# A two-layer mixer on one core: 128-row products in place of 32-column ones for the gate weights and the second layer's shift and scale, and a 128-row broadcast of the running maximum

## Chip, core and metric

The kernel runs on one core of a Trainium2 chip. The metric is the time of one execution on the device, in microseconds (us); for the kernel before the median of three runs is known. Besides that there is the trace of one profiled execution. The engines are named as in the profile: PE (TensorE, its products), PEld (TensorE, its weight loads), DVE (VectorE), ACT (ScalarE), POOL (GpSimd), SP (SyncE, which issues all DMAs of this kernel).

## What is computed

Two layers of a mixer over 512 tokens and 1024 channels, all in float32. Each layer normalises x, scales and shifts it by vectors that come from a condition c (`mod`), projects it to five groups of 1024 columns, runs a gated linear recurrence (RG-LRU) on two groups and a chunked mLSTM of four heads on the other three, and projects back. Cut to what the change touches:

```python
mod = c_act @ w_ada[l] + b_ada[l]
shift, scale, gate = jnp.split(mod, 3, axis=-1)
h = rms_norm(x, norm_g[l]) * (1.0 + scale[:, None, :]) + shift[:, None, :]
...
q = block_diag(xc, w_q)          # 4 heads, 256 x 256 each
k = block_diag(xc, w_k)
v = block_diag(xm, w_v)
gates = (jnp.concatenate([q, k, v], axis=-1) @ w_if + b_if)     # 3072 -> 8
...
m_t = jnp.maximum(m_inter, jnp.max(d, axis=-1))                 # running maximum of a head
w_intra = jnp.exp(d - m_t[..., None])
```

## The kernel before

**Precision.** Almost every product is made of three: an operand is split into a high and a low part of the type float32r (`whi` and `wlo` for weights, `hh` and `hl` for activations), and hi*hi, hi*lo and lo*hi are summed in PSUM (`mm3`). A few small products take plain float32 operands (`f32=True`); the trace has two weight loads and two products on PE for each of these.

**Order.** A planner records every instruction in the order in which the program traces it and then makes a list schedule: each engine serves what is due first, by costs and due times that the planner works out from assumed durations. The result is a fixed order on every engine. Each engine then runs its own list strictly in order, and waits where an operand isn't there yet or a buffer isn't free. The tile `raw` (a block of weights as it comes from memory, 512 KB) has three buffers, and the SP queue issues the next load when a buffer is free.

**Gate weights.** The gates need (w_q, w_k, w_v) @ w_if. For each of four heads `qk_weights` makes the tile `A` = w_q w_k^T (12 products of 256 columns), and beside it the gates' weights seen through w_q and w_k: 256 channels by 8. `v_gate_weights` does the same for w_v, two heads at a time. Before, the 8 columns of w_if are the stationary operand, padded with zeros to 32 columns (`wifpad`), and the 256 columns of `raw` are streamed. Four such products fill the four column quarters of the array (`tp=(0, 32 * q)`, tile `wqg` or `wvg`). Then `fold` copies the result to SBUF (`wfsb`, on DVE) and transposes and sums it with two further products by a selection matrix (`sela`, `selg`) into `wfT`, and DVE copies that to `wf`. `wf` is split and put beside other operands: as 8 more columns of `ph`/`pl` (for the scores `S`) and of `wvh`/`wvl` (for the values `v`).

**Second layer's shift and scale.** During `out` and `outq` (the output projection of layer 0) `mod_sum` sums two accumulators (`macc`, 128 rows by 1024 channels) over their rows: four products with 32 columns of ones as stationary operand into the four column quarters (`modps`), a copy (`modsb`), and two products by `sel4` (`modT`).

**Running maximum.** `ml_sw` spreads the running maximum of a head, which lies as hi and lo in rows 0 to 3 and 32 to 35 of `mhl`, over 128 rows by one product with `selh` (tile `Mbc`), using 36 rows of both operands. There are four per layer; two of them stand between products `oz` and two stand ahead of eight transposes `yT`.

**What follows what.** In layer 0 the program traces: `mx` (the mLSTM columns of the input projection), head 0's `qk_weights`, `v_gate_weights`, head 1's `qk_weights`, head 0's `p`, `v` and `S`, head 2's `qk_weights`, the last `mx`, and so on. Layer 1 is alike, with fewer `mx` ahead.

Of the kernel before, what the change touches and what calls it, by code (L numbers as in the profile page):

```python
# [30 lines left out]
# columns of the packed per-channel parameters  # L31
# [3 lines left out]
# what of adaLN is summed up on the vector engine: (layer, third)  # L35
# [3 lines left out]
# order of the rows of w_out: the mLSTM half first  # L39
CORD = list(range(8, 16)) + list(range(0, 8))  # L40
# where block j of the causal scores lies: (tile, first column)
# [4 lines left out]
class View:  # L46
    """A part of a logical tile; becomes an access pattern when its instruction is issued."""
# [60 lines left out]
class Planner:  # L108
    """Records instructions, then issues them on each engine in the order of a list schedule: the tensor
    engine follows the traced order, the others serve what it needs first."""  # L110
# [132 lines left out]
    def deadlines(self):  # L243
# [14 lines left out]
        # a PSUM bank is wanted again by a later tile; ready a little ahead of that  # L258
# [27 lines left out]
    def schedule(self):  # L286
# [4 lines left out]
        ready = {e: [] for e in engines}     # (late, i)  # L291
        events = []                          # (time, i): a finished instruction
        nfree = {k: [(0.0, s) for s in range(n)] for k, (n, _) in self.kinds.items()}
        # tiles still without a slot, by the deadline of their first use
# [18 lines left out]
        def fits(o):  # L313
            need = {}
            for b in o.tiles:
                if b.kind in self.kinds and b.slot is None:
                    need.setdefault(b.kind, []).append(b)
            for k, bs in need.items():
                room = len(nfree[k]) - len(bs)
                if room < 0:  # L320
                    return False
                # slots stay for the tiles that come before these
                ahead, w, h, last = 0, want[k], head[k], max(b.first for b in bs)
                while h < len(w) and w[h][0] < last:
                    if w[h][1].slot is None and w[h][1] not in bs:
                        ahead += 1
                        if ahead > room:
                            return False
                    h += 1
            return True  # L330

        def bank_free(o):
            # engines take turns at a PSUM bank
            return max((b.busy[1] for b in o.tiles if b.kind == "ps" and b.busy[0] != o.eng), default=0.0)
# [23 lines left out]
        while done < len(ops):  # L358
# [23 lines left out]
            # next time at which something changes  # L382
# [43 lines left out]
def trunk_kernel(ctx: ExitStack, tc: tile.TileContext, x, cT, params, bif, bgate, fg,  # L426
# [80 lines left out]
    # t < s: above any maximum, so that its exponential is 0; elsewhere below any  # L507
# [3 lines left out]
    # rows 32 q of four row groups; and pairs of groups, or all, row by row  # L511
    sel4, sel2, selg = keep("sel4", [128, 4]), keep("sel2", [128, 2]), keep("selg", [128, 16])
    sela, selm, selh = keep("sela", [128, 8]), keep("selm", [36, 4]), keep("selh", [36, 4, 128], F32R)

    def selectors():
        P.vcopy(sel4, ident[:, 0:128:32])
        P.tt(sel2, ident[:, 0:128:64], ident[:, 32:128:64], ALU.add)
        for n in range(2):
            P.tt(selg[:, 8 * n:8 * n + 8], ident[:, 64 * n:64 * n + 8], ident[:, 64 * n + 32:64 * n + 40], ALU.add)
        P.tt(sela, selg[:, 0:8], selg[:, 8:16], ALU.add)  # L520
        P.tt(selm, ident[0:36, 0:4], ident[0:36, 32:36], ALU.add)
        P.vcopy(selh, selm.spread(2, 128))
# [31 lines left out]
    def log1p_exp_neg(ab, shape):  # L554
        # log(1 + exp(-ab)) for ab >= 0: u = exp(-ab), 2 atanh(u / (2 + u))
# [23 lines left out]
    # 4 softplus(-lambda), and halves of the biases of the RG-LRU gates, for both layers  # L579
# [18 lines left out]
    def mod_first(d0, nd):  # L598
        # shift and scale of the first layer, channel blocks d0 .. d0 + nd
# [5 lines left out]
        for k in range(4):  # L605
            # quadrants: (which, half of the rows)
# [25 lines left out]
    def mod_units(l, w):  # L632
        # third w (shift, scale, gate) of layer l: products and sums over the blocks of rows, one step a block
# [11 lines left out]
    def mod_sum(l, w):  # L645
        # the sum over the rows of a block
# [14 lines left out]
        ps = bank("modps", (128, 256))  # L661
        for q in range(4):
            P.mm(ps[32 * q:32 * q + 32, :], ones[:, 0:32], acc[q // 2][:, 256 * (q % 2):256 * (q % 2) + 256], True,
                 True, tp=(0, 32 * q), f32=True)
        sb = slot("modsb", F32, (128, 256))
        P.vcopy(sb, ps)
        pt = bank("modT", (128, 4, 2))
        for c in range(2):
            P.mm(pt[:, :, c], sb[:, 128 * c:128 * c + 128], sel4, True, True, f32=True)
        pt = pt.chan(KC)  # L670
# [32 lines left out]
    def h_part(l, hT, xn, d0, nd, half):  # L703
        # channel blocks d0 .. d0 + nd of two token blocks, transposed, scaled, shifted, split
# [48 lines left out]
    def silu2(ps, name, shape=(128, 512)):  # L753
        # 2 silu
        th = slot(name + "t", F32, shape)
        P.act(th, ps, AF.Tanh, scale=0.5)
        P.stt(th, th, 1.0, ps, ALU.add, ALU.mult)
        return th

# [1 line left out]
    def gate_weights(l):  # L761
        raw = slot("wifraw", F32, (128, 24, 8))
        P.dma(raw, w_if[l], 98304)
        pad = [slot("wifpad", F32, (128, 16, 32)), slot("wifpadv", F32, (128, 8, 32))]
        for t, a, b in ((pad[0], 0, 16), (pad[1], 16, 24)):
            P.pool(lambda t=t: nc_g.memset(t.ap(), 0.0), [t], [], 0.4)
            P.vcopy(t[:, :, 0:8], raw[:, a:b, :])
        return pad

    def fold(ps, sel, n):  # L770
        # rows 32 q + g of ps, transposed and summed over the groups q that sel joins: [128, chunk, n]
        sb = slot("wfsb", F32, (128, 256))
        P.vcopy(sb, ps)
        pt = bank("wfT", (128, 2, n))
        for c in range(2):
            P.mm(pt[:, c, :], sb[:, 128 * c:128 * c + 128], sel, True, True, f32=True)
# [4 lines left out]
    def qk_weights(l, p, st):  # L781
        # A = w_q w_k^T, and the gates' weights seen through w_q and w_k
        raw = load_raw(w_qk[l, p], (2, 2, 256))
        ps = bank("wqg", (128, 256))
        for m in range(2):
            for ec in range(2):
                q = 2 * m + ec
                P.mm(ps[32 * q:32 * q + 32, :], st["pad"][0][:, 8 * m + 2 * p + ec, :], raw[:, m, ec, :], True, True,
                     tp=(0, 32 * q), f32=True)
# [9 lines left out]
        st["gq"][p] = fold(ps, sela, 8)  # L799

    def v_gate_weights(l, st):
        for u in range(2):
            raw = load_raw(w_vT[l, u], (2, 2, 256))
            ps = bank("wvg", (128, 256))
            for h in range(2):
                for ec in range(2):
                    q = 2 * h + ec
                    P.mm(ps[32 * q:32 * q + 32, :], st["pad"][1][:, 2 * (2 * u + h) + ec, :], raw[:, h, ec, :],
                         True, True, tp=(0, 32 * q), f32=True)
            st["gv"][u] = fold(ps, selg, 16)  # L810

    def v_weights(l, u, st):
        # w_v of two heads, with the gates' columns beside it
# [24 lines left out]
    def ml_head(l, p, st):  # L838
# [34 lines left out]
        # scores, transposed, times 16; the gates' columns follow the last token  # L873
# [32 lines left out]
    def gate_chain(l, st):  # L906
# [13 lines left out]
        # sums of log f inside the blocks, and the blocks' totals on every partition  # L920
# [4 lines left out]
        # a[i - j][:, j]: log i - b of block j, from where block i starts  # L925
# [23 lines left out]
        P.pool(lambda: nc_g.memset(mhl.ap()[0:36, :].bitcast(F32), 0.0), [mhl[0:36, :]], [], 0.3)  # L949
# [9 lines left out]
    def ml_oz(l, h, hT, st):  # L959
        # tanh(o / 2) and 2 silu(z) of a head, in two steps  # L960
# [19 lines left out]
    def ml_sw(h, st):  # L980
        # S * exp(a_s - M_t), causal, split
        pm = bank("Mbc")
        P.mm(pm, selh[:, h, :], st["mrow"][0:36, :], True, True)
# [74 lines left out]
    def rg_gates(l, g, st):  # L1058
# [4 lines left out]
        for cc in range(2):  # L1063
# [6 lines left out]
            # r2 = 2 sigmoid(p) = (1 + |tanh(p / 2)|) exp(min(p, 0)); s = -log a = 4 sp r2;  # L1070
            # 1 - a^2 = tanh(s) (1 + a^2)
# [36 lines left out]
    def out_evac(l, ps, xt, cs):  # L1108
        # x + gate * y
# [46 lines left out]
    def final_pre(xt):  # L1156
        # of the first 768 channels: squares summed, x times the final gain
# [34 lines left out]
    for l in range(L):  # L1192
# [14 lines left out]
        if l == 0:  # L1207
            def front(n):
                # a stage's shift and scale, then its part of h, between the products of the stage before
# [34 lines left out]
        st["pad"] = gate_weights(l)  # L1244
# [85 lines left out]
def _pack(inp):  # L1330
# [5 lines left out]
    def chan(v):  # [L, n * 128] -> [L, 128, n]  # L1336
# [7 lines left out]
    # adaLN, first layer's shift and scale: [channel block, k', p, quadrant, 128]; quadrant = (which, half of the rows)  # L1344
    wa = a["w_ada"].reshape(L, 2, 4, 128, 3, 8, 128)[0, :, :, :, 0:2]  # kh, k', p, which, block, n
    wa = wa.transpose(4, 1, 2, 3, 0, 5)  # block, k', p, which, half, n
# [4 lines left out]
    # o and z of a head side by side  # L1351
    oz = a["w_in"][:, :, 3072:].reshape(L, 4, 2, 128, 2, 4, 256)  # l, k pair, k, p, which, head, n
    w_oz = oz.transpose(0, 5, 1, 3, 2, 4, 6).reshape(L, 4, 4, 128, 1024)
    # transposed heads: l, h, m, e, d
# [7 lines left out]
    rg = np.stack([a["rg_w_a"], a["rg_w_x"]], axis=2)  # l, h, m, d, e  # L1362
# [32 lines left out]
```

## Time and profile before

| | us |
|---|---|
| median of three runs | 855.59 (854.89 to 856.32) |
| profiled execution, first to last instruction (span) | 853.5 |
| PE busy | 835.0 |
| DVE, ACT, POOL busy | 607.3, 476.7, 40.9 |

Of the profiled execution the span alone is known. The median stands 2.1 us over it; that is taken for what lies ahead of the first instruction and behind the last. Busy time counts an instruction from its start to its end, and matmuls overlap: what one costs on the path is the step from its start to the start of the next one.

### The profile page before, as it was taken

What the parts mean: (1) busy time and instruction counts of PE and PEld (TensorE: products, weight loads), DVE (VectorE), ACT (ScalarE), POOL (GpSimd) and SP (SyncE); (2) the same over time, 40 slices, a digit from 0 to 9 for tenths busy, and PEclk for the clock granted to TensorE, in tenths of its full rate; (3) what the DMA queues carried; (4) which work ended last, traced back from release to release, by engine and by line L of the source; (5) the groups of instructions that cost most, each with busy time, mean ns of one, the idle gap of its engine ahead of it and who ended that gap; (6) DMA issues with size and microseconds to landing.
All of it is one profiled execution on the core that took longest, in us unless ns stands there. A gap on an engine that the chain in (4) does not pass through costs nothing.

```text
span 853.5 us, 12548 instructions
## 1 busy us (share of the span) xinstructions
PE 835.0 (98%) x4664; PEld 698.1 (82%) x4664; DVE 607.3 (71%) x1227; ACT 476.7 (56%) x938; POOL 40.9 (5%) x66
## 2 busy tenths in 40 slices
PE   4999999999999999999999999999999999999996
PEld 3677897888888888887999789878888888888896
DVE  5467976898889699654466897376775877967643
ACT  4357763655457969622146766364454696893322
POOL 3000001011100000000010000100000000000000
PEclk9999999999999999999999999999999999999999
DMA  9924132466553323523231422033333222273202
GB/s 323 323 81 137 62 121 78 149 202 210 183 195 111 112 74 125 196 99 123 88 107 62 159 87 99 26 111 136 125 109 122 91 77 96 70 252 123 74 26 99
DMA packets 37053, 107.60 MB, mean 126 GB/s; under 512 B 4352, under 2 KB 6400, under 8 KB 36992
## 3 DMA queue, kind: packets, MB, share of 16 engines
q1 hardware_dynamic: 36992, 106.80, 36.2%
q8 instruction: 37, 0.61, 0.3%
q14 instruction: 24, 0.20, 0.1%
HBM read 102.58 MB, written 4.19 MB: 125 GB/s over the span
## 4 chain that ended last, share of the span: by engine, by line
PE 97%; DVE 1%; DMA 1%; POOL 1%; SPq 0%; ACT 0%; issue 0%; POOLq 0%
PE oz L153 20%; PE mx L153 11%; PE outq L153 11%; PE out L153 11%; PE rgz L153 10%; PE rgx L153 10%; PE S L153 4%; PE num L153 3%; PE v L153 3%; PE p L153 3%; PE A L153 2%; PE modps L153 2%; PE px L153 1%; PE pa L153 1%; PE hT L162 1%; PE yT L162 1%
## 5 line engine op out<-in xcount | busy, mean ns | idle before, releaser
L183 ACT CAST whi<-raw 128x1024 fp32r<-128x1024 f32 (+1 forms) x133 | 130.9, 994 | 186.7 <-PE oz L153 63.1
L190 DVE TENSOR_TENSOR wlo<-raw,whi 128x1024 fp32r<-128x1024 f32 (+1 forms) x133 | 151.9, 1148 | 72.4 <-ACT whi L183 72.0
L153 PE MATMUL oz<-whi,hh 128*128 128x512 f32 x256 | 101.8, 399 | 0.0
L153 PE MATMUL oz<-whi,hl 128*128 128x512 f32 x256 | 101.2, 395 | 0.0
L153 PE MATMUL oz<-wlo,hh 128*128 128x512 f32 x256 | 101.1, 395 | 0.0
L153 PE MATMUL outq<-whi,yh 128*128 128x256 f32 x256 | 72.5, 283 | 0.0
L153 PE MATMUL outq<-wlo,yh 128*128 128x256 f32 x256 | 72.4, 283 | 0.0
L153 PE MATMUL outq<-whi,yl 128*128 128x256 f32 x256 | 72.4, 283 | 0.0
L153 PE MATMUL mx<-hh,whi 128*128 128x512 f32 (+1 forms) x166 | 59.1, 358 | 0.0
L153 PE MATMUL mx<-hl,whi 128*128 128x512 f32 (+1 forms) x166 | 58.4, 352 | 0.0
L153 PE MATMUL mx<-hh,wlo 128*128 128x512 f32 (+1 forms) x166 | 57.4, 348 | 0.0
L153 PEld LDWEIGHTS oz<-whi,hh 128*128 128x128 f32 x256 | 48.1, 188 | 11.2 <-issue 1.0
L153 PEld LDWEIGHTS oz<-whi,hl 128*128 128x128 f32 x256 | 48.1, 188 | 11.1
L153 PEld LDWEIGHTS oz<-wlo,hh 128*128 128x128 f32 x256 | 48.1, 188 | 10.2
L153 PE MATMUL out<-whi,yh 128*128 128x512 f32 x128 | 50.6, 396 | 0.0
L153 PE MATMUL out<-whi,yl 128*128 128x512 f32 x128 | 50.6, 395 | 0.0
L153 PE MATMUL rgx<-hh,whi 128*128 128x512 f32 x128 | 50.5, 395 | 0.0
L153 PE MATMUL out<-wlo,yh 128*128 128x512 f32 x128 | 50.5, 394 | 0.0
L153 PE MATMUL rgz<-hh,whi 128*128 128x512 f32 x128 | 50.4, 394 | 0.0
L153 PE MATMUL rgz<-hl,whi 128*128 128x512 f32 x128 | 50.4, 394 | 0.0
L153 PE MATMUL rgx<-hl,whi 128*128 128x512 f32 x128 | 50.4, 394 | 0.0
L153 PE MATMUL rgz<-hh,wlo 128*128 128x512 f32 x128 | 50.4, 394 | 0.0
(256 smaller groups left out, 2029.7 us busy)
## 6 DMA issues: line engine op xcount, KB each, us to landing
raw<-in_w_in_dram SPq DMA_DIRECT2D x45, 512.0 KB, 3.2
raw<-in_w_oz_dram SPq DMA_DIRECT2D x32, 512.0 KB, 3.2
raw<-in_w_ada_dram SPq DMA_DIRECT2D x32, 512.0 KB, 3.3
raw<-in_w_out_dram SPq DMA_DIRECT2D x32, 512.0 KB, 3.2
wada<-in_w_adb_dram SPq DMA_DIRECT2D x24, 256.0 KB, 5.2
x<-in_x_dram SPq DMA_DIRECT2D x16, 256.0 KB, 5.5
raw<-in_w_qk_dram SPq DMA_DIRECT2D x8, 512.0 KB, 3.2
wada<-in_w_ada_dram SPq DMA_DIRECT2D x8, 256.0 KB, 4.3
```

The source lines that it names most:

```text
L153: self.nc.tensor.matmul(out.ap(), lhsT=lhsT.ap(), rhs=rhs.ap(), start=start, stop=stop, **kw)
L162: self.op("PE", lambda: self.nc.tensor.transpose(out.ap(), in_.ap(), ident.ap()), [out], [in_, ident], 0.109)
L183: self.op("ACT", lambda: self.nc.scalar.copy(out.ap(), in_.ap()), [out], [in_], 0.1 + 0.00084 * in_.n)
L190: self.op(eng, lambda: e.tensor_tensor(out=out.ap(), in0=a.ap(), in1=b.ap(), op=op), [out], [a, b], c)
```

## The change

Three things change; the diff is cut to its core (comments that go, and line numbers, are left out).

1. The gates' weights: the blocks of `raw` (128 by 128) become the stationary operand and the 8 columns of w_if are streamed, straight into the final layout (`seen`). The padding, the copy `wfsb`, and the products by `sela`/`selg` go. Each of the 12 groups (8 in `qk_weights`, 4 in `v_gate_weights`) now has 8 products of 8 columns, traced behind `A` and not ahead of it.
2. `mod_sum` for the second layer's shift and scale: 8 products with a block of the accumulator stationary and one column of ones streamed.
3. `Mbc` uses all 128 rows: `mhl` and `selh` are zero in the rows that are new.

```diff
-    sel4, sel2, selg = keep("sel4", [128, 4]), keep("sel2", [128, 2]), keep("selg", [128, 16])
-    sela, selm, selh = keep("sela", [128, 8]), keep("selm", [36, 4]), keep("selh", [36, 4, 128], F32R)
+    sel2, selm, selh = keep("sel2", [128, 2]), keep("selm", [128, 4]), keep("selh", [128, 4, 128], F32R)
...
     def selectors():
-        P.vcopy(sel4, ident[:, 0:128:32])
         P.tt(sel2, ident[:, 0:128:64], ident[:, 32:128:64], ALU.add)
-        for n in range(2):
-            P.tt(selg[:, 8 * n:8 * n + 8], ident[:, 64 * n:64 * n + 8], ident[:, 64 * n + 32:64 * n + 40], ALU.add)
-        P.tt(sela, selg[:, 0:8], selg[:, 8:16], ALU.add)
-        P.tt(selm, ident[0:36, 0:4], ident[0:36, 32:36], ALU.add)
+        P.tt(selm, ident[:, 0:4], ident[:, 32:36], ALU.add)
         P.vcopy(selh, selm.spread(2, 128))
...
     def mod_sum(l, w):
...
-        ps = bank("modps", (128, 256))
-        for q in range(4):
-            P.mm(ps[32 * q:32 * q + 32, :], ones[:, 0:32], acc[q // 2][:, 256 * (q % 2):256 * (q % 2) + 256], True,
-                 True, tp=(0, 32 * q), f32=True)
-        sb = slot("modsb", F32, (128, 256))
-        P.vcopy(sb, ps)
-        pt = bank("modT", (128, 4, 2))
-        for c in range(2):
-            P.mm(pt[:, :, c], sb[:, 128 * c:128 * c + 128], sel4, True, True, f32=True)
-        pt = pt.chan(KC)
+        pt = bank("modT", (128, KC))
+        for c in range(KC):
+            P.mm(pt[:, c:c + 1], acc[c // 4][:, 128 * (c % 4):128 * (c % 4) + 128], ones[:, 0:1], True, True, f32=True)
...
     def gate_weights(l):
         raw = slot("wifraw", F32, (128, 24, 8))
         P.dma(raw, w_if[l], 98304)
-        pad = [slot("wifpad", F32, (128, 16, 32)), slot("wifpadv", F32, (128, 8, 32))]
-        for t, a, b in ((pad[0], 0, 16), (pad[1], 16, 24)):
-            P.pool(lambda t=t: nc_g.memset(t.ap(), 0.0), [t], [], 0.4)
-            P.vcopy(t[:, :, 0:8], raw[:, a:b, :])
-        return pad
-
-    def fold(ps, sel, n):
-        sb = slot("wfsb", F32, (128, 256))
-        P.vcopy(sb, ps)
+        return raw
+
+    def seen(raw, parts, wif, n):
         pt = bank("wfT", (128, 2, n))
-        for c in range(2):
-            P.mm(pt[:, c, :], sb[:, 128 * c:128 * c + 128], sel, True, True, f32=True)
+        for dc in range(2):
+            for col, blocks in parts:
+                for i, (idx, row) in enumerate(blocks):
+                    P.mm(pt[:, dc, col:col + 8], raw[:, idx[0], idx[1], 128 * dc:128 * dc + 128], wif[:, row, :],
+                         i == 0, i == len(blocks) - 1, f32=True)
         t = P.tile("gw", (128, 2, n), F32, "wf")
         P.vcopy(t, pt)
         return t
...
     def qk_weights(l, p, st):
         raw = load_raw(w_qk[l, p], (2, 2, 256))
-        ps = bank("wqg", (128, 256))
-        for m in range(2):
-            for ec in range(2):
-                q = 2 * m + ec
-                P.mm(ps[32 * q:32 * q + 32, :], st["pad"][0][:, 8 * m + 2 * p + ec, :], raw[:, m, ec, :], True, True,
-                     tp=(0, 32 * q), f32=True)
...
-        st["gq"][p] = fold(ps, sela, 8)
+        st["gq"][p] = seen(raw, [(0, [((m, ec), 8 * m + 2 * p + ec) for m in range(2) for ec in range(2)])],
+                           st["wif"], 8)
...
-            st["gv"][u] = fold(ps, selg, 16)
+            st["gv"][u] = seen(raw, [(8 * h, [((h, ec), 16 + 2 * (2 * u + h) + ec) for ec in range(2)])
+                                     for h in range(2)], st["wif"], 16)
...
         mhl = slot("mhl", F32R)
-        P.pool(lambda: nc_g.memset(mhl.ap()[0:36, :].bitcast(F32), 0.0), [mhl[0:36, :]], [], 0.3)
+        P.pool(lambda: nc_g.memset(mhl.ap().bitcast(F32), 0.0), [mhl], [], 0.5)
...
-        P.mm(pm, selh[:, h, :], st["mrow"][0:36, :], True, True)
+        P.mm(pm, selh[:, h, :], st["mrow"], True, True)
```

The change also moves instructions, since the planner's due times shift. The first place is PE in layer 0, between the last `mx` and the `v` of head 0. Before, the quarter products stand between those of `A` (a row is one instruction, or several alike; the number of columns stands at its end, ahead of it the rows of the result):

```order
L153 MATMUL A<-whi,wlo 128x256
L153 MATMUL A<-whi 128x256
L153 MATMUL wvg<-raw,wifpadv 32x256
L153 MATMUL A<-wlo,whi 128x256
L153 MATMUL wvg<-raw,wifpadv 32x256
L153 MATMUL A<-whi,wlo 128x256
L153 MATMUL wvg<-raw,wifpadv 32x256 x2
L153 MATMUL wfT<-sela,wfsb 128x8 x2
L153 MATMUL wqg<-raw,wifpad 32x256 x4
L153 MATMUL A<-whi 128x256
L153 MATMUL A<-wlo,whi 128x256
L153 MATMUL wfT<-selg,wfsb 128x16 x2
```

Now head 0's `A` runs through, 16 `wfT` follow (head 0's and the first pair of values'), then head 1's `A`, and at its end this:

```order
L153 MATMUL A<-whi 128x256
L153 MATMUL A<-wlo,whi 128x256
L153 MATMUL A<-whi,wlo 128x256
L153 MATMUL wfT<-wifraw,raw 128x8 x8
L153 MATMUL p<-xch,Ah 128x512
L153 MATMUL p<-xcl,Ah 128x512
L153 MATMUL p<-xch,Al 128x512
L153 MATMUL wfT<-wifraw,raw 128x8 x8
L153 MATMUL p<-xch,Ah 128x512
L153 MATMUL p<-xcl,Ah 128x512
L153 MATMUL p<-xch,Al 128x512
```

The first 8 `wfT` here are head 1's; the second 8 are those of the second pair of values, and they stand three products into `p`; nine more `p` and four `v<-wvh` follow, then two `S`, and then the first product that reads `wvl`.

The second place is DVE over the same stretch. Before, the last copies `wf` and what follows them, up to the split of w_v (`wvl<-raw`), stand so:

```order
L213 COPY wfsb<-wvg 128x256
L213 COPY wf<-wfT 128x32
L198 SCALAR_TENSOR_TENSOR xcl<-msilut,xch 128x512
L190 TENSOR_TENSOR xml<-xmf,xmh 128x512
L213 COPY wf<-wfT 128x32
L190 TENSOR_TENSOR Al<-A,Ah 128x512
L213 COPY wf<-wfT 128x16
L190 TENSOR_TENSOR pl<-wf,ph 128x8
L190 TENSOR_TENSOR wvl<-raw,wvh 128x4x256
```

Now three steps of a convolution (`mconv`) stand between the last `wf` and `wvl<-raw`:

```order
L190 TENSOR_TENSOR Al<-A,Ah 128x512
L213 COPY wf<-wfT 128x16
L190 TENSOR_TENSOR pl<-wf,ph 128x8 x2
L198 SCALAR_TENSOR_TENSOR mconv<-xmf,par,mconv 128x511
L213 COPY wf<-wfT 128x32
L198 SCALAR_TENSOR_TENSOR mconv<-xmf,par,mconv 128x510 x2
L198 SCALAR_TENSOR_TENSOR mconv<-xmf,par,mconv 128x509
L190 TENSOR_TENSOR wvl<-raw,wvh 128x4x256
```

The second `wf` here copies what those second 8 `wfT` on PE make, and the three convolution steps and `wvl<-raw` are queued behind it.

## Rows read from the trace of the kernel before

**Rows 1.** The page: span, and the chain that ended last by engine.
```profile
span 853.5 us, 12548 instructions
...
PE 97%; DVE 1%; DMA 1%; POOL 1%; SPq 0%; ACT 0%; issue 0%; POOLq 0%
```

**Rows 2.** Timeline of PE at head 2 of layer 0 (start, length, instruction).
```profile
84.74 0.28 PE L153 MATMUL S<-ph,xcl 128*128 128x264 f32 x1
84.95 0.64 PE L153 MATMUL wqg<-raw,wifpad 128*32 128x256 f32 x8
...
85.75 0.28 PE L153 MATMUL A<-wlo,whi 128*128 128x256 f32 x1
...
87.53 0.39 PE L153 MATMUL mx<-hh,wlo 128*128 128x512 f32 x1
...
88.44 0.39 PE L153 MATMUL mx<-hl,whi 128*128 128x512 f32 x1
```

**Rows 3.** Timeline of PE, first groups of layer 0: first and last.
```profile
64.47 0.39 PE L153 MATMUL mx<-hh,wlo 128*128 128x512 f32 x1
...
76.17 0.40 PE L153 MATMUL p<-xch,Ah 128*128 128x512 f32 x1
...
77.56 0.39 PE L153 MATMUL p<-xcl,Ah 128*128 128x512 f32 x1
```

**Rows 4.** Timeline of PE, first groups of layer 1: first and last.
```profile
465.69 0.28 PE L153 MATMUL mx<-hh,wlo 128*128 128x256 f32 x1
...
474.64 0.39 PE L153 MATMUL mx<-hl,whi 128*128 128x512 f32 x1
```

**Rows 5.** Timeline of PE around the two sums of `mod_sum`.
```profile
387.09 0.40 PE L153 MATMUL out<-whi,yl 128*128 128x512 f32 x1
...
390.26 0.28 PE L153 MATMUL outq<-whi,yh 128*128 128x256 f32 x1
...
401.20 0.28 PE L153 MATMUL outq<-whi,yl 128*128 128x256 f32 x1
...
404.77 0.28 PE L153 MATMUL outq<-wlo,yh 128*128 128x256 f32 x1
...
405.36 0.28 PE L153 MATMUL outq<-whi,yh 128*128 128x256 f32 x1
```

**Rows 6.** Timeline of PEld, the loads of one fold and the load behind.
```profile
71.83 0.53 PEld L153 LDWEIGHTS wfT<-selg,wfsb 128*128 128x128 f32 x4
72.28 0.19 PEld L153 LDWEIGHTS A<-whi,wlo 128*128 128x128 f32 x1
```

**Rows 7.** Timeline of PE at two `Mbc`, and at transposes without one ahead.
```profile
147.61 0.40 PE L153 MATMUL oz<-whi,hl 128*128 128x512 f32 x1
147.94 0.50 PE L153 MATMUL Mbc<-mhl,selh 36*128 36x512 f32 x1
...
148.70 0.39 PE L153 MATMUL oz<-wlo,hh 128*128 128x512 f32 x1
...
182.29 0.39 PE L153 MATMUL oz<-whi,hl 128*128 128x512 f32 x1
...
183.89 0.48 PE L153 MATMUL oz<-whi,hh 128*128 128x512 f32 x1
...
237.11 1.03 PE L162 MATMUL yT<-ident,tmp 128*128 128x128 f32 x8
237.90 0.47 PE L153 MATMUL rgx<-hh,whi 128*128 128x512 f32 x1
```

**Rows 8.** Timeline of DVE: a copy `wf`, the split of w_v, five convolution steps.
```profile
76.04 0.19 DVE L213 COPY wf<-wfT 128x32 f32<-128x32 f32 x1
...
76.90 1.21 DVE L190 TENSOR_TENSOR wvl<-raw,wvh 128x1024 fp32r<-128x1024 f32 x1
...
86.15 3.38 DVE L198 SCALAR_TENSOR_TENSOR mconv<-xmf,par,mconv 128x510 f32<-128x510 f32 x5
```

**Rows 9.** The page's DMA issues: one kind of block (KB, us to landing).
```profile
raw<-in_w_qk_dram SPq DMA_DIRECT2D x8, 512.0 KB, 3.2
```

More of the change, by code (lines that the diff above doesn't have):

```diff
@@ L803, in v_gate_weights @@
             raw = load_raw(w_vT[l, u], (2, 2, 256))
[L804 to L809, printed above, removed]
-            st["gv"][u] = fold(ps, selg, 16)
+            st["gv"][u] = seen(raw, [(8 * h, [((h, ec), 16 + 2 * (2 * u + h) + ec) for ec in range(2)])
+                                     for h in range(2)], st["wif"], 16)
     def v_weights(l, u, st):
@@ L1243, in trunk_kernel @@
             ml_head_pre(l, p, ps01[p], st)
-        st["pad"] = gate_weights(l)
+        st["wif"] = gate_weights(l)
         qk_weights(l, 0, st)
```

## The prediction

> **What bounds the kernel now.** I read the page first. The span is 853.5 us, and of the chain of work that ended last 97% lies on PE [rows 1]: the kernel is one queue of products, and whatever the change does to the time it does through PE's queue, or by making that queue wait. So the next view is PE's timeline around each place that the diff touches. What is to be seen there is not the length of a row but the step from its start to the next start, since products overlap. An undisturbed product of 512 columns takes a step of 0.232 us (76.17 to 77.56 is six steps) [rows 3], one of 256 columns 0.118 us (404.77 to 405.36 is five) [rows 5]. In proportion one of 264 columns takes 0.122 us. Everything beyond these steps is what the touched products cost, the delay of their neighbours included.
>
> **The gate weights, before.** There are two kinds of place. At head 2 of layer 0 the four quarter products stand together: from 84.74 to 85.75 is 1.01 us, in which one product of 264 and one of 256 columns also run, so 1.01 - 0.122 - 0.118 = 0.77 us for the quarters. The fold stands between `mx`: 87.53 to 88.44 is 0.91 us, less two products of 512 is 0.45 us [rows 2]. Together 1.22 us. Five of the fourteen groups stand so (heads 2 and 3 of layer 0, heads 1 to 3 of layer 1): 6.10 us.
>
> The other groups are interleaved with full-width products, and every change over costs. In layer 0, from 64.47 to 76.17 there are 11.70 us; besides four groups (heads 0 and 1, both pairs of values) the stretch holds 24 products of `A` (2.83) and five of 512 columns (1.16), so the four groups cost 7.71 us [rows 3]. In layer 1, from 465.69 to 474.64 there are 8.95 us with three groups, 13 products of 256 (1.53) and four of 512 (0.93): 6.49 us [rows 4].
>
> `mod_sum`: 387.09 to 390.26 is 3.17 us less four products of 512 = 2.24 us; 401.20 to 404.77 is 3.57 us less five of 256 = 2.98 us [rows 5]. Each is followed by a fold like that of [rows 2], 0.45 us. Together 6.12 us. All fourteen groups: 6.10 + 7.71 + 6.49 + 6.12 = 26.42 us.
>
> **The gate weights, after.** The trace has no run of 16 loads with 8 columns streamed behind each, but it has one of four. A plain float32 product is two loads and two products, and four loads of a fold take from 71.83 to 72.28, 0.1125 us each, though a load alone lasts 0.19 [rows 6]; the fold of [rows 2] gives 0.45 / 4 = 0.112. I take 0.112, so a group of 8 products costs 16 x 0.112 = 1.79 us and the fourteen 25.06 us. The step is set by the load, so one column (`mod_sum`) costs what 8 do. The bounds are 0.110 and 0.1125, 0.5 us in all. So the groups that stood together lose 0.57 us each, and those that were interleaved gain. The sum is 25.06 - 26.42 = **-1.36 us**: the larger part of the edit is nearly a wash.
>
> **The broadcast.** `Mbc` between `oz`: 147.61 to 148.70 is 1.09 us less two products of 512 = 0.63 us. Ahead of transposes: 182.29 to 183.89 is 1.60 us, less one product (0.232) and the eight transposes, which take 0.79 where nothing of this kind stands ahead (237.11 to 237.90), = 0.58 us [rows 7]. A product of 512 columns that is like its neighbours takes 0.232, and a sum over 128 rows takes PE no longer than one over 36 (the columns set the step). Four of each: 4 x (0.63 - 0.232) + 4 x (0.58 - 0.232) = 1.59 + 1.39 = **-2.98 us**. The lower bound is nothing: the row shows that the product before `Mbc` and the one behind are late too, not why. What the row shows is 36 rows against 128 and a step of 0.43 (147.94 on) where 0.232 is usual [rows 7]. The Trainium skill, TensorEngine Tiling (Array Packing), "Key Properties", says that a change of tiling mode drains TensorE; if 36 rows are run as a mode of 64 rows, the drains on both sides go with this edit, and by that the whole 2.98 us come. I take the whole, since `Mbc` reads alike between `oz` and ahead of `yT`, and since the quarter products, which use a part of the array too, make the product before them late in the same way (84.74 to 84.95 is 0.21 where 0.122 is usual) [rows 2].
>
> **What else goes or moves.** DVE loses 14 copies (`wfsb`, `modsb`) and four of the padding, POOL four fills; both lie beside PE's queue, and none is the last thing that PE waits for in these stretches, so they are worth nothing directly. The longer fill of `mhl` and the cast of `selh` work on more rows with the same columns, beside PE. The list of SP: a buffer of `raw` is now held until `wfT` has read it, and that stands behind `A`. In layer 0 the second block of w_v^T waits for head 0's `wfT`: 64.47 + 0.232 + 12 x 0.118 + 1.79 = 67.91, and lands 3.2 us later [rows 9], at 71.1. By the order after, PE wants it at 67.91 + 1.79 + 1.42 + 1.79 + 0.70 = 73.6. So 2.5 us cover it. The block of w_v behind it is issued at 69.7 and lands at about 73. Later blocks have more time.
>
> **A new wait.** After those 8 `wfT` (73.60 to 75.39) PE does nine `p` (2.09), four `v` (0.49) and two `S` (0.24), and at 78.21 wants `wvl`. On DVE the copy `wf` can't start before about 75.54 (0.15 behind the last load; this is an estimate). Behind it in the same list stand three convolution steps and then `wvl<-raw`. By the rows: `wf` 0.15 of its 0.19, 3.38 / 5 = 0.68 for each convolution step, 1.21 for the split [rows 8], so 75.54 + 0.15 + 2.03 + 1.21 = 78.93. PE waits **+0.72 us**. The bounds are 0.3 (steps of 0.55) and 1.2. Elsewhere what stands behind a `wf` is wanted later: in layer 1 48 products `mx` (11 us) follow the three groups, and behind `mod_sum` the next weights of `outq` are wanted some 50 products on.
>
> **Sum.** -1.36 - 2.98 + 0.72 = -3.6 us, 0.42%. On the profiled execution that is a span of 849.9; its time is the span and 2.1 us around it if it ran like the median, and nothing that the change touches lies there. So the median goes from 855.6 to **852.0 us**. What a measurement of this kernel can tell from no change is about 0.2%, 1.7 us.
>
> **Rivals.**
> - *No new wait, or almost none* (0.13): DVE is quicker than assumed, and the time is 851.3 us. For it: the 3.38 us also hold the tail of the last step, so that a step may be nearer 0.6, and `wf` may start a little sooner than I put it.
> - *The broadcast keeps its drains* (0.08): they come from the product's waits, not from its 36 rows. Then -1.36 + 0.72 is left, 855.0 us. Against it: `oz` and `yT`, with other things awaited, show the same step.
> - *DVE's list becomes a chain of waits* (0.14): each of the twelve `wf` makes DVE wait for PE's longer run, and what is queued behind is late for PE. Without waits the gain is 4.3 us; 0.36 us at each of the twelve eats it, and 0.50 each makes the kernel slower by more than 0.2%. If all twelve cost what I find for the one, 12 x 0.72 = 8.6, the time is 859.9 us. Against it: DVE has idle time and less work, and at ten of the twelve I find nothing wanted soon. For it: the planner places these copies by its own costs, and gives a small product 0.12 us where the rows have 0.22.
> - *The loads don't overlap in a long run* (0.02): then each of the 224 loads costs its 0.19 and not 0.112 [rows 6], +17.5 us, 869.5 us. It decides from 0.128 each on (3.6 / 224 more). The Trainium skill, TensorE: Matmul & The Clock Gate, "The mechanism", says that loads overlap running products only where the row group differs; here it is the same for all, so by that rule this rival holds, and the trace disagrees: loads start 0.112 apart.
>
> **How the numbers follow.** The forecast has 0.60; the rest, 0.03, is what I haven't thought of. The forecast's own range is 850.9 to 853.3: 0.5 for the load step, 0.5 for the wait, and the scatter of a median. To hold 8 in 10 the range must reach over the lucky case below and the drains case above: **850.6 to 855.0**. Faster by over 0.2% (below 853.9): nearly all of the forecast and the first rival, 0.59 + 0.13 + a little of the others = 0.76. Within 0.2%: the drains case and most of the chain case that is small, 0.08 + 0.09 + 0.01 = 0.18. Slower: 0.06.
>
> **What would show each step.** In the changed kernel's timeline: the runs of `wfT` at 1.79 us for 8 products, and no delay of the product ahead; `Mbc` with 128 rows at a step of 0.232 and the following `oz` at 0.232; the products `v<-wvl` of layer 0 near 78.9 with a gap of about 0.7 ahead, and DVE's `wvl` as its releaser; 1.8 us for each `modT`. PE without other new gaps after 15 us. The prediction is wrong if gaps ahead of PE appear at other groups, if the step of a small product is over 0.128, or if `Mbc` stays at 0.43.

## The result, and the profile of the changed kernel

The changed kernel is slower. Five executions took 858.30 to 863.07 us, median 862.56; the kernel before, beside it, has a median of 855.92. The ratio is 1.0062, with a 95% interval of 1.0039 to 1.0085. The prediction was 852.0, with a range that ended at 855.0. One execution among those below, of experiment 8, took 1379.93 us at a mean clock of 0.56, and the number given there leaves it out.

The profiled execution took 863.07 us, its span is 861.4, 7.9 more than before [rows 1]. The page shows where to look: the row of the granted clock, a digit for each fortieth of the span. Before, all forty digits are 9:

```profile
PEclk9999999999999999999999999999999999999999
```

After, two are not: the slices from 64.6 and from 473.8 us.

```profile
span 861.4 us, 12622 instructions
...
PE   4999999999999999999999999999999999999996
...
PEclk9996999999999999999999799999999999999999
```

PE's own row shows nothing there: it is busy all the time. The view by windows gives the clock of a stretch (behind the five busy times). It is 0.50, that is 1.2 GHz and not 2.4, from 71.57 to 85.22 us and from 474.35 to 484.58 us:

```profile
core 0: us, PE busy (x) PEld busy (x) DVE busy (x) ACT busy (x) POOL busy (x), PEclk, DMA share, GB/s
60.00:71.50 11.50, 11.50 (x78) 10.46 (x77) 10.39 (x17) 10.11 (x18) 0.10 (x1) 1.00 0.14 45
71.57:85.20 13.63, 13.63 (x54) 12.47 (x53) 5.83 (x13) 5.12 (x11) 0.00 (x0) 0.50 0.40 126
...
474.35:484.50 10.15, 10.15 (x37) 9.02 (x37) 7.80 (x17) 6.68 (x13) 0.10 (x1) 0.50 0.49 165
```

PE's timeline in layer 0 (start, length, instruction, count) shows what stood ahead of the fall and what it cost:

```profile
66.97 3.63 PE L153 MATMUL wfT<-wifraw,raw 128*128 128x8 f32 x32
70.45 0.36 PE L153 MATMUL A<-whi 128*128 128x256 f32 x1
...
72.24 3.42 PE L153 MATMUL wfT<-wifraw,raw 128*128 128x8 f32 x16
75.50 0.77 PE L153 MATMUL p<-xch,Ah 128*128 128x512 f32 x1
...
80.77 0.63 PE L153 MATMUL p<-xcl,Ah 128*128 128x512 f32 x1
81.20 0.63 PE L153 MATMUL p<-xch,Al 128*128 128x512 f32 x1
...
85.38 0.29 PE L153 MATMUL v<-wvl,xmh 128*128 128x264 f32 x1
```

Sixteen products `wfT` (32 instructions, since each plain float32 product is two) take from 66.97 to 70.45: 3.48 us, 1.74 a group of eight, near the 1.79 predicted. The clock falls 1.1 us later, within `A`. From then on the next eight take 3.26 us (72.24 to 75.50), and a product of 512 columns takes a step of 0.43 and not 0.232 [rows 3]. In layer 1 the clock falls inside a row of 24:

```profile
471.64 7.77 PE L153 MATMUL wfT<-wifraw,raw 128*128 128x8 f32 x48
...
479.26 0.77 PE L153 MATMUL mx<-hh,whi 128*128 128x512 f32 x1
...
484.52 0.44 PE L153 MATMUL mx<-hh,whi 128*128 128x512 f32 x1
484.80 0.39 PE L153 MATMUL mx<-hl,whi 128*128 128x512 f32 x1
```

The 24 take 7.62 us where 5.4 were expected, and `mx` is back at full speed only from 484.52 on. The two stretches hold 13.65 + 10.24 = 23.9 us at half clock; half of that, 11.9 us, is about what they can have cost (an estimate: it takes every step there as twice as long, where the steps read above went from 0.232 to 0.43). The five groups of 8 that stand alone in the same kernel (from 92.91, 116.86, 494.32, 507.08 and 531.03 us) take 1.70 us each, at full clock. All five executions say the same: the three near 863 us have a mean clock of 0.985, the two of 858.30 one of 0.990.

The other two edits came as foretold. These rows answer to [rows 7] and [rows 5]:

```profile
156.50 0.40 PE L153 MATMUL oz<-whi,hl 128*128 128x512 f32 x1
156.73 0.39 PE L153 MATMUL Mbc<-mhl,selh 128*128 128x512 f32 x1
156.96 0.40 PE L153 MATMUL oz<-whi,hh 128*128 128x512 f32 x1
...
395.17 1.84 PE L153 MATMUL modT<-ones,macc 128*128 128x1 f32 x16
396.87 0.36 PE L153 MATMUL outq<-whi,yh 128*128 128x256 f32 x1
397.07 0.28 PE L153 MATMUL outq<-wlo,yh 128*128 128x256 f32 x1
```

`Mbc` has a step of 0.23 where it had 0.43, and neither neighbour is late. From `modT` to the second `outq` behind it is 1.90 us, of which one product of 256 columns is 0.12.

### The profile page after: what moved, and what is told of

Same layout as the page of the kernel before. It is cut to its first block, busy times and chain, and to the rows that moved or that the text cites. A ratio compares the mean times of both kernels' runs of the same rounds, so it can differ in the third digit from the quotient of the medians.

```text
span 861.4 us, 12622 instructions
## 1 busy us (share of the span) xinstructions
PE 840.6 (98%) x4720; PEld 721.7 (84%) x4720; DVE 601.2 (70%) x1205; ACT 476.0 (55%) x938; POOL 40.3 (5%) x62
## 4 chain that ended last, share of the span: by engine, by line
PE 95%; DVE 2%; POOL 1%; DMA 1%; ACT 0%; issue 0%; SPq 0%; POOLq 0%; ACTq 0%
PE oz L153 19%; PE mx L153 11%; PE outq L153 11%; PE rgx L153 10%; PE out L153 10%; PE rgz L153 10%; PE S L153 3%; PE num L153 3%; PE wfT L153 3%; PE p L153 3%; PE v L153 3%; PE A L153 1%; PE px L153 1%; PE pa L153 1%; PE modps L153 1%; POOL u L190 1%
## 5 line engine op out<-in xcount | busy, mean ns | idle before, releaser
L153 PE MATMUL rgx<-hh,wlo 128*128 128x512 f32 x128 | 50.5, 394 | 0.0
```

Of the source, the lines that this page charges most:

```text
L153: self.nc.tensor.matmul(out.ap(), lhsT=lhsT.ap(), rhs=rhs.ap(), start=start, stop=stop, **kw)
```

## The experiments

Each was timed in turn with the kernel before, whose median lay between 855.5 and 856.2 us.

**1. The other two edits alone.** The kernel before, with only these lines (and `selm`, `selh` and the fill of `mhl` at 128 rows):

```diff
-        P.mm(pm, selh[:, h, :], st["mrow"][0:36, :], True, True)
+        P.mm(pm, selh[:, h, :], st["mrow"], True, True)
...
+        pt = bank("modT", (128, KC))
+        for c in range(KC):
+            P.mm(pt[:, c:c + 1], acc[c // 4][:, 128 * (c % 4):128 * (c % 4) + 128], ones[:, 0:1], True, True, f32=True)
```

> The kernel before with the 128-row Mbc and the new mod_sum; the gate weights stay as they were. Theory (the granted clock fell to half because of the long runs of wfT): no run of more than 8 such products is left, so the clock stays at 1.0 from 20 to 849 us, and both terms of the prediction come whole: 855.9 - 2.98 for Mbc - 2.54 for mod_sum (6.12 less 2 x 1.79) = 850.4 us, between 849.8 and 851.2. Rival one (something else in the change lowers the clock, such as the 128-row product or modT): the two stretches at half clock stay, 857 us or more. Rival two (no clock, but waits from the changed order of the other engines): between 851 and 856, with gaps ahead of PE that the kernel before doesn't have.

Measured: 852.0 us, ratio 0.995 (0.9937 to 0.9962); the clock is 1.0 from 21.4 to 847.4 us. So the loss is not in these edits. Both terms came in the trace (each sum 1.79 us; `Mbc` with its neighbours' delay 0.23 to 0.24, eight times), yet the median fell by 3.9 and not by 5.5. In the profiled execution a wait for a block of `wada` at the start is 1.1 us longer than before (4.89 against 3.82), which is a part of the difference; the rest isn't placed.

**2. The gate weights alone**, on the kernel before.

> The kernel before with the new gate weights alone; Mbc and mod_sum stay as they were. Theory (clock): both stretches at half clock stay, near 72 and near 475 us. The twelve groups themselves cost 12 x 1.79 = 21.5 where they cost 20.3, +1.2, and the two stretches some 6 to 12, so 855.9 + 1.2 + 6 to 12 = 863 to 869 us. Rival (the time was lost in the other two edits): 857 us, and a clock of 1.0 throughout.

Measured: 865.34 us, ratio 1.0109 (1.0093 to 1.0125). Half clock from 75.98 to 82.81 and from 478.75 to 482.17 us in the profiled execution, which at 863.39 is the fastest of four (mean clock 0.992; the others have 0.986 to 0.988):

```profile
76.00:82.70 6.70, 6.70 (x24) 5.83 (x24) 4.44 (x7) 2.22 (x4) 0.00 (x0) 0.50 0.54 172
478.80:482.10 3.30, 3.30 (x9) 2.62 (x9) 3.30 (x9) 2.99 (x5) 0.10 (x1) 0.50 0.83 276
```

The loss belongs to the gate weights. In this execution the clock did not fall behind the row of 16 products, which ended at 71.00, but inside the second of the two groups of 8 that follow (from 72.50 and 74.97); behind the row of 24, which ended at 478.74, it fell at once.

**3. The same instructions, traced apart.** `qk_weights` and `v_gate_weights` no longer call `seen`; it is called later, one group at a time:

```diff
         qk_weights(l, 1, st)
+        v_seen(l, 0, st)
         ml_head(l, 0, st)
+        qk_seen(1, st)
         qk_weights(l, 2, st)
```

> The changed kernel with its twelve groups of wfT traced apart: never more than 8 products wfT in a row, and between two groups at least 12 products of A or p; the same instructions otherwise. Theory (clock, through the runs of 16 and of 24 small products): no stretch at half clock, 862.6 less some 10 to 12, that is 851 to 853 us. Rival one (each group of 8, or the sum of them, is enough): half clock in at least one place, 857 us or more. Rival two (the time is lost in waits of DVE's list): the clock stays at 1.0 and the time is still above 856.

Measured: 852.75 us, ratio 0.9962 (0.995 to 0.9974), the clock 1.0 from 19.3 to 848.8 us. The line of the windows view for nearly all of that:

```profile
20.00:848.70 828.70, 822.36 (x4656) 705.46 (x4644) 589.99 (x1153) 467.96 (x915) 30.60 (x44) 1.00 0.37 122
```

The same products, with the same loads, lose nothing when no more than eight stand in a row and at least twelve wider products stand between two groups. This order also has the wait that the prediction put at 0.72 us:

```profile
74.49 0.40 PE L153 MATMUL S<-ph,xch 128*128 128x256 f32 x2
75.60 0.39 PE L153 MATMUL v<-wvl,xmh 128*128 128x264 f32 x1 [0.71 <-DVE wvl L190]
```

**4. The changed order, with wider products.** PE's loads and its order stay (but for one product `v` that moves by a few places), rows of 16 and 24 too; what differs is the columns streamed (the further 120 are discarded; `c` keeps the planner's cost at what it was), and beside PE a small fill on GpSimd and, for the values' groups, two copies `wf` for one, which moves DVE's list by one convolution step:

```diff
-        pt = bank("wfT", (128, 2, n))
+        pt = bank("wfT", (128, 2, n // 8, 16, 8))
...
-                    P.mm(pt[:, dc, col:col + 8], raw[:, idx[0], idx[1], 128 * dc:128 * dc + 128], wif[:, row, :],
-                         i == 0, i == len(blocks) - 1, f32=True)
+                    P.mm(pt[:, dc, col // 8], raw[:, idx[0], idx[1], 128 * dc:128 * dc + 128], wif[:, row:row + 16, :],
+                         i == 0, i == len(blocks) - 1, f32=True, c=0.12)
```

> The changed kernel in its own order, with each product wfT streaming 128 columns (the 8 that count and 120 that nobody reads) and not 8: the same 16 loads a group and the same runs of 16 and 24 products, but 16 times the columns streamed. Theory in the form 'it is the few streamed columns that let the clock fall': no stretch at half clock; a group still costs about 1.79 us, or up to 1.9 if the products set the step, so 851.5 to 854 us. Theory in the form 'it is the row of loads, or the plain float32 products, whatever they stream': half clock in the same two places, 858 to 864 us.

Measured: 853.13 us, ratio 0.9965 (0.9952 to 0.9979). By windows over the rows of 16, 8 and 24 products the clock is whole, and PE's timeline shows the 24 at 5.28 us:

```profile
66.27:69.70 3.43, 3.43 (x33) 3.43 (x32) 3.43 (x7) 3.35 (x6) 0.10 (x1) 1.00 0.15 39
71.26:72.90 1.64, 1.64 (x17) 1.64 (x16) 0.62 (x2) 1.44 (x5) 0.00 (x0) 1.00 0.64 170
465.50:470.80 5.30, 5.30 (x49) 5.30 (x49) 3.75 (x9) 5.29 (x12) 0.00 (x0) 1.00 0.38 111
```
```profile
78.49 0.39 PE L153 MATMUL v<-wvl,xmh 128*128 128x264 f32 x1
...
465.55 5.52 PE L153 MATMUL wfT<-wifraw,raw 128*128 128x128 f32 x48
470.83 0.48 PE L153 MATMUL mx<-hh,whi 128*128 128x512 f32 x1
...
473.71 0.40 PE L153 MATMUL mx<-hh,whi 128*128 128x512 f32 x1
```

Sixteen times the columns cost nothing, and gave back 9.4 us. From the start of the 24 to the thirteenth `mx` behind them it is 8.16 us here (465.55 to 473.71) and 12.88 in the changed kernel (471.64 to 484.52); from the 16 of layer 0 to the first `v<-wvl` 12.22 (66.27 to 78.49) and 18.41 (66.97 to 85.38). That is 4.72 + 6.19 = 10.9 us of the 9.9 between the two spans; the rest of the two spans makes up the 1.0 in between, and it lies scattered.

**5 and 6. A row of 24 in another place.** In the kernel before, in the output projection of layer 0, far from any gate weight:

```diff
+            if l == 0 and u == 3:
+                dm = bank("extra")
+                for i in range(24):
+                    P.mm(dm[:, 0:8], tri, ones[:, 0:8], True, True, f32=True, c=0.12)
```

> The kernel before, with 24 further plain float32 products put into the output projection of layer 0 (a block of constants stationary, 8 columns of ones streamed, written to a PSUM tile that nobody reads), more than 200 us away from any gate weight; a row of 24 as in the changed kernel's layer 1. Theory (a row of such products lets the granted clock fall, wherever it stands): the row itself costs 24 x 0.224 = 5.4 us, and a stretch at half clock begins inside it or just behind it and costs 2 to 6 more: 863 to 867 us. Rival (the clock falls through something of the gate weights' own place, such as the loads of raw or the other engines there): no such stretch, 855.9 + 5.4 = 861.3 us.

> The same row of 24 further products in the same place, each with 128 columns streamed and not 8. Theory: the clock stays at 1.0 and the row costs what its loads cost, 5.4 us, or up to 0.24 a product: 861.3 to 861.9 us. Rival (any long row of plain float32 products does it): a stretch at half clock here too, 863 us or more.

Measured: 864.33 us with 8 columns (five executions, 861.96 to 865.22; ratio 1.0096, 1.0083 to 1.0108), 861.18 with 128 (860.29 to 861.56; 1.0059, 1.0046 to 1.0071). PE's timeline, with 8:

```profile
364.56 5.42 PE L153 MATMUL extra<-ones,tri 128*128 128x8 f32 x48
369.84 0.67 PE L153 MATMUL out<-whi,yh 128*128 128x512 f32 x1
...
372.87 0.63 PE L153 MATMUL out<-wlo,yh 128*128 128x512 f32 x1
373.30 0.44 PE L153 MATMUL out<-whi,yl 128*128 128x512 f32 x1
373.57 0.39 PE L153 MATMUL out<-whi,yh 128*128 128x512 f32 x1
```

And with 128:

```profile
365.74 5.52 PE L153 MATMUL extra<-ones,tri 128*128 128x128 f32 x48
371.02 0.48 PE L153 MATMUL out<-whi,yh 128*128 128x512 f32 x1
371.33 0.39 PE L153 MATMUL out<-wlo,yh 128*128 128x512 f32 x1
```

Both rows take 5.28 us. Only the one with 8 columns is followed by products at half clock, 3.4 us of them in this execution, the fastest of its five. The windows view, with 8 and with 128:

```profile
370.00:373.30 3.30, 3.30 (x9) 2.54 (x10) 0.00 (x0) 0.00 (x0) 0.00 (x0) 0.50 0.49 153
```
```profile
371.00:400.00 29.00, 29.00 (x141) 22.66 (x140) 11.61 (x16) 6.99 (x12) 0.00 (x0) 1.00 0.30 103
```

So a row of 24 with few columns does it by itself, in another place, with other weights and other work around it. A row of 16 alone was not tried.

**7. The quarter products of before, undivided.** With the new `Mbc` and `mod_sum`, the four quarter products and the two products of a fold each become one unit of the planner (`mms` issues a list of products as one instruction of the plan):

```diff
+        P.mms([(ps[32 * (2 * m + ec):32 * (2 * m + ec) + 32, :], st["pad"][0][:, 8 * m + 2 * p + ec, :],
+                raw[:, m, ec, :], (0, 32 * (2 * m + ec))) for m in range(2) for ec in range(2)])
```

> The gate weights as they were before (four quarter products and a fold), but each four, and each two of a fold, issued as one unit of the planner, so that no full-width product can come between them; Mbc and mod_sum as changed. Theory (what made the groups of before dear is the change between quarter products and full-width ones, each way): the seven groups that were interleaved come from 14.20 us (7.71 and 6.49) to 7 x 1.22 = 8.54, so 852.0 - 5.7 = 846.3 us, between 845.5 and 848; no run of small products is long, the clock stays at 1.0. Rival (those places are slow through waits for copies and loads): 851 to 852 us as in the first experiment.

Measured: 847.35 us, ratio 0.9902 (0.9887 to 0.9918). Each four now costs 0.76 us, and each fold 0.45 where PE does not wait, in both layers, as the standing-together groups of [rows 2] did; so it was standing between full-width products that made the others dear. Less than the 5.7 us came, for PE now reaches folds ahead of their copies:

```profile
463.28 0.61 PE L165 MATMUL wfT<-sela,wfsb 128*128 128x8 f32 x4 [0.27 <-DVE wfsb L222]
...
465.50 0.59 PE L165 MATMUL wfT<-selg,wfsb 128*128 128x16 f32 x4 [1.04 <-DVE wf L222]
```

A third wait, 0.54 us, stands in layer 0, and behind it the clock was at half for 3.4 us (72.61 to 76.03) in the profiled execution. I had expected 1.0 throughout.

**8. GpSimd's power, in the kernel of experiment 4.**

```diff
         P.ts(ng, ab, -1.0, ALU.mult)
+        if shape == (4, 4):
+            o = P.ops[-1]
+            P.ts(sm("spare", shape), ab, 1.0, ALU.mult)
+            P.ops[-1].behind = o
```

> The kernel of the fourth experiment (changed order, 128 columns streamed) with one small DVE instruction that nobody needs put behind ng of the gate chain, ahead of DVE's next split. In all kernels so far the power on GpSimd that follows ng took 3.98 us where DVE's split of two operands had started some 10 ns ahead of it, and 2.91 us where it started 50 to 300 ns behind it; PE then waited 1.1 us for lf, ahead of cumb, or not at all. Theory (the power loses the race for something it shares with DVE): 2.9 us in both layers, no wait ahead of cumb, 853.1 - 2.2 = 850.9 us, between 850.3 and 851.6. Rival (its duration comes from its data or from what GpSimd did before): 3.98 us still, and 853.1 us.

Measured: 852.05 us (the median of five executions, 851.12 to 853.78), ratio 0.9962 (0.995 to 0.9974), no change that can be told from experiment 4. The added instruction was too short: in layer 0 DVE's split still started 10 ns ahead of the power, in layer 1 it came 56 ns behind. So the two layers of one execution show both cases. GpSimd's power, then DVE's split beside it:

```profile
132.93 3.98 POOL L191 TENSOR_TENSOR u<-ec,ng 128x16 f32<-128x16 f32 x1 [15.91 <-DVE spare L207]
...
543.05 2.91 POOL L191 TENSOR_TENSOR u<-ec,ng 128x16 f32<-128x16 f32 x1 [15.84 <-DVE spare L207]
```
```profile
132.92 1.23 DVE L191 TENSOR_TENSOR wlo<-raw,whi 128x1024 fp32r<-128x1024 f32 x1
...
543.10 1.25 DVE L191 TENSOR_TENSOR wlo<-raw,whi 128x1024 fp32r<-128x1024 f32 x1
```

PE waited 1.1 us ahead of `cumb` in layer 0 and not at all in layer 1.

**9. Experiment 7 with folds later.** The folds are traced behind the next group of large products, and the small instruction of experiment 8 is in:

```diff
         if npre == 2:
             ml_head_pre(l, 2, chan_group(l, 10, hT, ("mx0", "mx1")), st)
+            folds("gq", 0)
+            folds("gv", 0, 1)
```

> The kernel of the seventh experiment (quarter products of before, issued together; new Mbc and mod_sum), with the same small DVE instruction, and with the folds of the groups traced some 2 us or more behind their quarter products, so that PE does not stand before a fold until its copy is there. In the seventh experiment PE waited 0.54 us in layer 0 and 0.27 + 1.04 in layer 1 for these copies, and 1.1 us ahead of cumb in layer 1, and the clock was at half for 3.4 us behind the waiting place in layer 0. Theory: all of it goes, 847.35 - 1.85 - 1.1 - up to 1.7 = 842.7 to 844.4 us. Rival (the waits go elsewhere, the half clock stays): 845 to 847 us.

Measured: 846.98 us, ratio 0.9897 (0.9882 to 0.9911): the rival's case. The wait ahead of `cumb` is gone (the split came 300 and 365 ns behind the power, which took 2.91 both times), and the clock is 1.0 from 19.7 to 842.3 us; but the order has waits of its own:

```profile
PE v L153 <- ACT S L185: 0.9, 2, 0.4
PE S L153 <- DVE pl L199: 0.7, 1, 0.7
PE wfT L165 <- DVE wfsb L222: 0.5, 1, 0.5
```

(Engine, line, what it waited for: us in total, times, longest.) This and experiment 7, which differ by less than they scatter, are the fastest here: 8.6 to 8.8 us below the kernel before and 15 below the changed one.

## Why the prediction was wrong

*The step that failed* is "a group of 8 products costs 16 x 0.112 = 1.79 us and the fourteen 25.06". Taken by itself it holds: in experiment 4 the fourteen cost 25.0 us. But it prices a group as if it stood alone, and carried the 0.112 over from a row of four loads to rows of 32 and 48; what such a row does to the products behind it was put at nothing, without a reason. The order after showed these rows of 16 and 24 products, and the bounds that were set ("0.110 and 0.1125") asked only whether a load would stay as quick, never whether the clock would stay. What the runs showed in its place is half clock in and behind these rows, 23.9 us of it in the profiled execution of the changed kernel. No rival had a clock at 1.2 GHz; it lay in the 0.03 for what wasn't thought of. Experiments 3 to 6 show the cause: long rows of products, each with two loads and 8 columns, are followed or cut by half clock, in three places (a row of 24 in two of them, in the third a row of 16 and two of 8 close behind); set apart, or with 128 columns, they are not. How long a row may be isn't shown, beyond that 8 did no harm. What it cost is 862.56 - 853.13 = 9.4 us, by experiment 4.

*The gate weights at full clock*: a near wash as predicted, so without the clock the edit would still have been worth little.

*The broadcast*: right in mechanism and size. By step the eight cost 4.82 us before and 1.91 in experiment 4, -2.91 where -2.98 was foretold.

*`mod_sum`*: 1.79 us each, as foretold.

*The new wait on `wvl`*: 0.71 us where it came (experiment 3), but only 0.15 in experiment 4 (the split ended at 78.44, PE wanted it at 78.34), since there two convolution steps and not three stood behind `wf`. In the changed kernel the half clock hid it: three steps stood there, the split ended at 83.69, and PE came to it at 85.38. So the changed order at full clock, with its three steps, was not measured.

*A wait that was not foretold*: 1.1 us ahead of `cumb` in layer 0, which before had it in layer 1 alone. The rows of the changed kernel, and GpSimd's power in the gate chain ahead of it, before and after:

```profile
132.79 2.90 POOL L190 TENSOR_TENSOR u<-ec,ng 128x16 f32<-128x16 f32 x1 [13.09 <-DVE ng L206]
```
```profile
140.67 3.99 POOL L190 TENSOR_TENSOR u<-ec,ng 128x16 f32<-128x16 f32 x1 [15.94 <-DVE ng L206]
...
147.60 0.37 PE L153 MATMUL cumb<-lf,tri 128*128 128x16 f32 x2 [1.10 <-DVE lf L198]
```

Experiment 4 has the same wait in both layers. By the terms, then, it should stand 1.4 + 2.9 - 0.15 - 1.1 = 3.1 us below before; the medians say 2.8, the spans 2.0. Against experiment 4 the forecast's 852.0 would have been 1.1 too low, within its range; part of that nearness is luck, since the wait on `wvl` was put 0.57 too high for it and the 1.1 ahead of `cumb` at nothing.

*The rivals*: "the loads don't overlap in a long run" came nearest, since it looked at the length of the rows; but it named another mechanism, and 17.5 us. "DVE's list becomes a chain of waits" did not happen: no group's copy held PE in the changed kernel.

## What to carry to other kernels

When a change makes products narrow, look in the new order for how many of them stand in a row, and read the granted clock beside PE's busy time: PE reads as busy in a row of loads with 8 columns each. Two remedies cost nothing here: set such groups apart between wide products, or let them stream more columns while the load sets the step (here up to 128). And a product that uses part of the array is cheap beside its like and dear between full-width ones, so issue them together.

## What the runs showed of the hardware

**PE's clock fell without a wait of PE.** In the changed kernel no gap of PE over 0.1 us lies between 20 and 134 us, yet the clock fell at 71.57. It did not come back with the first wide products either (12 `mx` behind the row of 24, at steps of 0.43 after the first). The Trainium skill, TensorE: Matmul & The Clock Gate, "HAM oscillation — how this bites in real kernels", lays a clock that falls in mid-kernel to waits between bursts; here it fell in and behind rows without a wait. Experiment 7's fall, behind a wait of 0.54 us among quarter products and folds, was not taken apart.

**A power on GpSimd took longer where a split on DVE had just started.** In all eleven kernels traced, the power of the gate chain took 3.97 to 3.99 us where a split on DVE had started up to 15 ns ahead of it, and 2.90 to 2.91 where the split started 50 ns or more behind: 22 of 22 times. The 1.07 us between them is most of the split's 1.23. Each layer shows both durations (layer 0 has 2.90 before and 3.99 in the changed kernel, layer 1 3.98 before and 2.91 in experiment 3), so it isn't the data. The Trainium skill, SBUF — State Buffer, "SBUF: two separate sides", says that GpSimd shares a pair of ports with DVE, which an instruction of DVE with two SBUF inputs holds from start to end. For the power the trace agrees; the page also says that the one that starts second is blocked, and there it does not: a split that starts 50 ns behind the power takes 1.25 us and not 2.9. That the order of the two starts is the cause was not forced cleanly (experiment 8 moved one layer of two).
